# Output projection: normalized rows transposed by VectorE in squares and scaled by ScalarE, the norm's factors put into W_ff1's rows, three pairs of loads on GpSimd's queue

## The chip, the cores and the metric

One core of one Trainium2 chip runs the whole layer as a single program. The metric is the device time of one execution in microseconds. A core has five engines that run side by side and wait for each other through semaphores: TensorE (PE; PEld is its loading of weights), VectorE (DVE), ScalarE (ACT), GpSimd (POOL) and SyncE (SP). SP issues most of the DMAs, GpSimd and ScalarE some; each of the three issues them in the order of its own queue.

## The reference, cut to what matters

The model dimension is 1024, there are 2048 tokens, the MLP is 4096 wide, and all is float32.

```python
def rmsnorm(x, g):
    y = x * lax.rsqrt(jnp.mean(x * x, axis=-1, keepdims=True) + EPS)
    return y * g

# nx = rmsnorm(x, attn_norm_g); mixed = [gated linear attention ; dilated attention] of nx
h = x + einsum('bsm,md->bsd', mixed, w_out)
nm = rmsnorm(h, mlp_norm_g)
a = square(relu(einsum('bsd,df->bsf', nm, w_ff1)))
h = h + einsum('bsf,fd->bsd', a, w_ff2)
out = rmsnorm(h, final_norm_g)
```

The change touches the second and third lines: how `nm` comes from `h`, how it is turned so that the model dimension lies on the partitions, and where `mlp_norm_g` is multiplied in. Since `nm @ w_ff1` sums over the model dimension, the factor `mlp_norm_g[d]` can be applied to column d of `nm` or to row d of `w_ff1`.

## The kernel before, in words

The kernel goes through the layer in stages: input projection, both attention mixers, output projection, first MLP product (FF1), second MLP product (FF2). Two things are done in every large product. First, each float32 operand is split into a high part of type fp32r and the rest: ScalarE copies the operand into `hi`, VectorE subtracts (`split`, lines 542 to 544), and three matmuls are added up in PSUM (`mm3`, lines 139 to 142). Second, the products are not done block by block: block sums of both operands are formed, and seven block products take the place of eight (in the input projection, the output projection and FF1; FF2 has a larger scheme). The numbers j = 1 to 7 name the block products, and the tuple `order` their order.

**Output projection** (from line 1674). Two 128-token tiles make a pair p; the pairs of the first token half come first. The first four tiles are multiplied plainly (`for at in range(4)`, line 1676), the other pairs by seven block products each (`for g in range(14, 56)`, line 1709; `prep0` splits the left operand three products ahead into one of four buffers `combs0`, and `product0` multiplies and adds the result to the rows `xhs[p]` that were loaded with x). The right operands are W_out and block sums of it. `mix_wo(c)` (line 1267) loads four of those sums from `wtD` into `wtraw` in two DMAs on SP's queue and splits them.

When a tile of rows is complete, `row_done` stores it to `hD` and puts `norm_row` on a list, and after every second tile `norm_sums` as well; `next_norm` takes one of the list at fixed places of the loops. `norm_row` (lines 1410 to 1422) has ScalarE square the row into the scratch `scr` with the sum accumulated, and make 1/rms of it by two small functions (`rstd_of`). VectorE then multiplies the row in place by 1/rms and by `gM`, the factors `mlp_norm_g` spread over all partitions. TensorE transposes the eight 128x128 blocks through the identity into two PSUM banks, and ScalarE copies each bank into `bb`. `store_T` sends blocks to `hTD` on SP's queue. `norm_sums` forms the block sums of two tiles on VectorE, in place of rows that are no longer needed, and stores them too.

**The first MLP product** (from line 1887). The tokens are taken in two halves. `token_pieces` (line 1436) brings a half back from `hTD` in 14 pieces of 512 KB, always four pieces ahead, each by one DMA on SP's queue into `rb`, and splits it into the `hb` tiles: the first half while the output projection ends, the second in the middle of FF1. W_ff1 comes in 32 groups of 256 columns (16 groups, once for each half). `load_w1(g)` loads a group in two DMAs on GpSimd's queue, the first two groups at g = 49 and g = 53 of the output projection. `jobs1` lists the pairs (group, j), seven jobs a group: mostly two groups after each other, in three places two groups interleaved (`mixed`). For each job, `prep1` runs two jobs ahead: it splits a block of the weights into one of the four `combs0` and lets VectorE form the block sums; `product1` does twelve matmuls (four `mm3`) and takes the result out of PSUM, by ScalarE alone for j = 1, 6, 5 and 4, and by a VectorE sum for j = 2, 7 and 3; ScalarE then applies relu and square. `some_sums` forms VectorE's sums for FF2 and stores them to `actD`.

**What sets the order.** The order of the instructions on each engine in these stages is planned by the framework at build time: among the instructions that its model of time holds to be ready, it takes the one that was written first. A call of `keep_in_program_order` fixes an instruction behind the one that was written just before it for the same engine. Tiles named by `slot` share 25 buffers of SBUF; a new one waits until the last user of the one before it in that buffer is done.

The input projection already has what the change uses: `squares` (line 605) transposes 32x32 squares on VectorE, `both_halves` gives views of the result, `load_turned` (line 612) loads one half of a turned block by four DMAs of 32 partitions each, alternately on SP's and GpSimd's queue, and `split_turned` (line 619) splits such a piece into its place. The 32x32 squares alone do not move data between groups of 32 partitions; that is done by these loads.

Of the kernel before, what the change touches and what calls it, by code (L numbers as in the profile page):

```python
# [10 lines left out]
F32 = mybir.dt.float32  # L11
FR = mybir.dt.float32r
I32 = mybir.dt.int32
AF = mybir.ActivationFunctionType
OP = mybir.AluOpType
# [3 lines left out]
D = 1024  # L19
NT = S // 128  # L20
HT = NT // 2
CH = D // 128
# [92 lines left out]
def emit(tc, a, stop=99):  # L115
    nc = tc.nc
    V, A, G, T, SP = nc.vector, nc.scalar, nc.gpsimd, nc.tensor, nc.sync
# [6 lines left out]
    def ps(tag):  # L124
        return psum.tile([128, 512], F32, name="ps_" + tag, tag=tag, bufs=BANKS[tag])

    def slot(name, dt=F32, n=SLOT):

        return up.tile([128, SLOT], dt, name=name, tag="u", bufs=25)[:, :n]

    def view(t, shape):
        n = int(np.prod(shape))
        names = "abcd"[:len(shape)]
        return t[:, :n].rearrange(f"p ({' '.join(names)}) -> p {' '.join(names)}", **dict(zip(names, shape)))

    def bcast_row(ap, n):
        return bass.AP(tensor=ap.tensor, offset=ap.offset, ap=[[0, 128], [1, n]])
# [12 lines left out]
    ident = const.tile([128, 128], F32, name="ident")  # L150
# [69 lines left out]
    boD = [[dram.tile([S, 132], F32, name=f"boD{p}_{b}") for b in range(2)] for p in range(4)]  # L220
    mixD = dram.tile([S, D], F32, name="mixD")
    hD = dram.tile([S, D], F32, name="hD")
    hTD = dram.tile([2, 7, 128, 4, 512], F32, name="hTD")
    actD = dram.tile([NPH, 128, 8, 2, 256], F32, name="actD")
    rowD = dram.tile([8, 3, 384], F32, name="rowD")
    rbD = [dram.tile([8, 128, 384], F32, name=f"rbD{d}") for d in range(3)]
# [315 lines left out]
    def split(hi, lo, src):  # L542
        A.activation(hi, src, AF.Copy)  # L543
        V.tensor_tensor(lo, src, hi.bitcast(F32), op=OP.subtract)  # L544
# [60 lines left out]
    def squares(dst, src):  # L605

        V.transpose(dst.rearrange("p (g c t) -> p g c t", g=4, t=32), src.rearrange("p (c g t) -> p g c t", g=4, t=32))

    def both_halves(v):
        return [v.rearrange("p (g k n) -> p k g n", g=4, k=2)[:, k] for k in range(2)]  # L610

    def load_turned(dst, src, n):

        for g in range(4):
            at = bass.AP(tensor=src.tensor, offset=src.offset + 128 * g + n * 8 * 32 * 512,
                         ap=[[512, 32], [32 * 512, 8], [1, 128]])
            (SP, G)[g % 2].dma_start(view(dst[32 * g:32 * g + 32], (8, 128)), at)

    def split_turned(parts_, src, n, pin=False):

        hi, lo = [v[:, :2048].rearrange("p (c b t) -> p b c t", c=4, t=32)[:, 8 * n:8 * n + 8] for v in parts_]
        r = view(src, (8, 4, 32))
        ins = A.activation(hi, r, AF.Copy)
        if pin:
            tc.keep_in_program_order(ins)
        V.tensor_tensor(lo, r, hi.bitcast(F32), op=OP.subtract)
# [640 lines left out]
    def mix_wo(c):  # L1267

        raw = slot("wtraw")
        for k in range(2):  # L1270
            SP.dma_start(raw[:, D * k:D * k + D], wtD[c, :, D * k:D * k + D])
        for k, j in ((1, 5), (3, 6), (2, 4), (0, 7)):
            split(*block_view(j, c), raw[:, 512 * k:512 * k + 512])

# [122 lines left out]


    gs, bb = slot("gs"), slot("bb")
    gM, scr = gs[:, :D], gs[:, D:2 * D]  # L1400
    hb4 = [view(bb[:, 512 * q:], (4, 128)) for q in range(4)]
    rb, TF, TB = [], {}, {}
    norms = []

    def store_T(t, *which):
        half, i = t // HT, t % 4
        for j, q in which:
            SP.dma_start(hTD[half, j - 1][:, :, i * 128:i * 128 + 128], hb4[q] if isinstance(q, int) else q)

    def norm_row(h, t):  # L1410

        ss = stat()
        A.activation(scr, h, AF.Square, accum_out=ss)
        r = rstd_of(ss, D)
        V.scalar_tensor_tensor(h, h, r, gM, op0=OP.mult, op1=OP.mult)
        k = t % HT // 4
        for q in range(2):
            pv = view(ps("c"), (4, 128))
            for c in range(4):
                T.transpose(pv[:, c], h[:, (4 * q + c) * 128:(4 * q + c + 1) * 128], ident)  # L1420
            A.activation(hb4[2 * k + q], pv, AF.Copy)
        store_T(t, *(((1, 0), (2, 1)) if k == 0 else ((3, 3),)))

    def norm_sums(t, x):
# [11 lines left out]
    def token_pieces(half, first, pace):  # L1436

        parts_at = {}
        for n in range(14):
            parts_at.setdefault(first + n * pace // 100, []).append(n)  # L1440
        piece = lambda n: rb[n // 2 % 2][:, 1024 * (n % 2):1024 * (n % 2) + 1024]

        def load(n):
            if n < 14:
                SP.dma_start(piece(n), hTD[half, order[n // 2] - 1][:, 2 * (n % 2):2 * (n % 2) + 2].rearrange("p c s -> p (c s)"))

        def step(at):
            if at == first - 4:
                while len(rb) < 2:
                    rb.append(slot("rb"))  # L1450
                for n in range(4):
                    load(n)
            for n in parts_at.get(at, ()):
                j = order[n // 2]
                if j not in TF:
                    TF[j] = [slot(f"hb{j}", FR) for _ in range(2)]
                    TB[j] = [view(v, (4, 512)) for v in TF[j]]
                cs = slice(1024 * (n % 2), 1024 * (n % 2) + 1024)
                split(*[v[:, cs] for v in TF[j]], piece(n))
                load(n + 4)  # L1460

        return step
# [34 lines left out]
    apart = [(g, j) for g in range(2) for j in order]  # L1497
    mixed = [(0, 1), (0, 2), (0, 6), (1, 1), (0, 5), (1, 2), (0, 7), (1, 6), (0, 3), (1, 5), (0, 4), (1, 7), (1, 3), (1, 4)]
    jobs1 = [(g + n, j) for g in range(0, 2 * NP, 2) for n, j in (mixed if g in (0, NP - 2, NP) else apart)]
    raw1, acc1 = [], []  # L1500

    def load_w1(g, halves=(0, 1)):
        if g < 2 * NP:
            if len(raw1) < 2:
                raw1.append(view(slot("w1raw"), (CH, 256)))
            g0 = g % NP * 256
            for k in halves:
                G.dma_start(raw1[g % 2][:, 4 * k:4 * k + 4], w1[:, 4 * k:4 * k + 4, g0:g0 + 256])  # L1508

    def prep1(at):  # L1510

        if at >= len(jobs1):
            return
        g, j = jobs1[at]
        r = raw1[g % 2]
        (a11, a12), (a21, a22) = [[r[:, 4 * k:4 * k + 4, n * 128:n * 128 + 128] for k in range(2)] for n in range(2)]
        c = combs0[at % 4]
        split(c[:, 0], c[:, 1], {1: a11, 2: a12, 6: a11, 5: a21, 7: a11, 3: a12, 4: a22}[j])
        if j == 2:
            V.tensor_tensor(a21, a21, a22, op=OP.add)  # L1520
            V.tensor_tensor(a11, a21, a11, op=OP.subtract)
            V.tensor_tensor(a12, a12, a11, op=OP.subtract)
        if j == 6:
            V.tensor_tensor(a11, a22, a11, op=OP.subtract)
        if j in (7, 4):
            load_w1(g + 2, (0,) if j == 7 else (1,))
# [149 lines left out]
    for at in range(4):  # L1676
        p, e = divmod(at, 2)
        m = nxt
        if at == 0:
            load_x(0, True)  # L1680
            tc.keep_in_program_order(SP.dma_start(gM, bcast_row(a["mlp_norm_g"], D)))
        if at in (0, 2):
            nxt = plain_rows(p, 1)
            load_mix(p + 1)
            load_x(p + 1)
        if at == 1:
            nxt = plain_rows(1, 0)
        mix_wo(at)
        if at == 3:
            for n in range(4):  # L1690
                raw_block(2, n % 2, n // 2)
            load_mix(3)
            for g in range(14, 16):
                prep0(g)
        b = [ps("ad"[e]), ps("ad"[e])]
        parts_ = 2 if at < 2 else 1
        for q in range(parts_):
            for n in range(2):
                for c in range(q * CH // parts_, (q + 1) * CH // parts_):
                    mm3(b[n], m[:, 0, c], m[:, 1, c], *wo_part(((1, 12), (2, 3))[c // 4][n], c % 4), c == 0, c == CH - 1)  # L1700
                if q == parts_ - 1:
                    x = xhs[p][:, e, 512 * n:512 * n + 512]
                    V.tensor_tensor(x, b[n], x, op=OP.add)
        next_norm()
        row_done(p, e)
        if at == 3:
            prep0(16)
    half0, half1 = token_pieces(0, -6, 110), token_pieces(1, 7 * (NP - 2) + 3, 130)
    for g in range(14, 56):
        p, i = divmod(g, 7)  # L1710
        prep0(g + 3)
        product0(g)
        if i in (0, 1, 5):
            next_norm()
        if i == 2:
            load_x(p + 1)
            raw_block(p + 1, 0, 0)
            raw_block(p + 1, 1, 0)
        if i == 3:
            raw_block(p + 1, 0, 1)  # L1720
        if i == 4:
            raw_block(p + 1, 1, 1)
            load_mix(p + 2)
        half0(g - 56)
        if g in (49, 53):
            load_w1(int(g > 49))
        if g >= 54:
            prep1(g - 54)

    w2 = a["w_ff2"].rearrange("o (c p) n -> p (o c) n", p=128)  # L1730
# [262 lines left out]
```

## Time and profile before

| | us |
|---|---|
| median of 3 runs | 2223.89 (2220.23 to 2224.09) |
| the profiled execution | 2219.28 |
| its span | 2217.1 |
| output projection with its norms (rough, from the windows) | 855 to 1060 |
| FF1 | 1023 to 1648 |
| FF2 | 1648 to 2217 |

The profile is of one execution, and its times are counted from the start of its span. A busy time adds up the instructions of an engine with overlaps counted once. Matmuls overlap in the trace, so the step from one start to the next tells what one of them costs in TensorE's queue, and its duration does not. A row such as `L1420 PE ...` names the line in the kernel, the engine, the operation, and the tiles as out<-in. In brackets, or in lists of waits, stands who ended an engine's idle time. A helper that records all splits has one line (L543 for ScalarE, L544 for VectorE), so these are told apart by their tiles: `mcomb<-w1raw` is a split of W_ff1, `hb<-rb` one of the tokens, `wb<-wtraw` one of W_out's sums.

### The profile page before, as it was taken

What the parts mean: (1) busy time and instruction counts of PE and PEld (TensorE: products, weight loads), DVE (VectorE), ACT (ScalarE), POOL (GpSimd) and SP (SyncE); (2) the same over time, 40 slices, a digit from 0 to 9 for tenths busy, and PEclk for the clock granted to TensorE, in tenths of its full rate; (3) what the DMA queues carried; (4) which work ended last, traced back from release to release, by engine and by line L of the source; (5) the groups of instructions that cost most, each with busy time, mean ns of one, the idle gap of its engine ahead of it and who ended that gap; (6) DMA issues with size and microseconds to landing.
All of it is one profiled execution on the core that took longest, in us unless ns stands there. A gap on an engine that the chain in (4) does not pass through costs nothing.

```text
span 2217.1 us, 34928 instructions
## 1 busy us (share of the span) xinstructions
PE 2198.8 (99%) x12356; PEld 1910.1 (86%) x12356; DVE 1662.0 (75%) x3100; ACT 1231.3 (56%) x2406; POOL 604.8 (27%) x653
## 2 busy tenths in 40 slices
PE   9999999999999999999999999999999999999998
PEld 8988998899999998888888888888888888888886
DVE  8677766757777887769776778767786697576788
ACT  7364424537888884547555566555555433333446
POOL 1000300135577672000000000000008443042672
PEclk9999999999999999999999999999999999999999
DMA  6576965777967976868654456555499998677875
GB/s 208 174 218 209 253 204 187 241 243 266 313 231 229 293 262 232 264 212 273 187 167 133 150 180 182 156 177 155 133 299 279 305 297 273 213 258 244 270 263 183
DMA packets 325074, 499.88 MB, mean 225 GB/s; under 512 B 21479, under 2 KB 226938, under 8 KB 313636
## 3 DMA queue, kind: packets, MB, share of 16 engines
q1 hardware_dynamic: 285426, 336.35, 46.8%
q0 software_dynamic: 32128, 108.61, 17.2%
q10 hardware_dynamic: 7346, 52.70, 6.4%
q8 instruction: 97, 1.59, 0.3%
q14 instruction: 77, 0.63, 0.1%
HBM read 339.45 MB, written 162.85 MB: 227 GB/s over the span
## 4 chain that ended last, share of the span: by engine, by line
PE 76%; issue 12%; DMA 4%; DVE 4%; ACT 2%; POOL 1%; SPq 1%; DVEq 0%; POOLq 0%; ACTq 0%
PE ps_a L141 7%; PE ps_a L140 7%; PE ps_a L142 7%; PE ps_c L141 7%; PE ps_c L140 7%; PE ps_c L142 7%; PE ps_a L1021 4%; PE ps_d L141 4%; PE ps_d L142 4%; PE ps_d L140 4%; PE ps_o L140 3%; PE ps_o L141 3%; PE ps_o L142 3%; PE ps_d L1002 3%; PE ps_c L984 2%
## 5 line engine op out<-in xcount | busy, mean ns | idle before, releaser
L543 ACT ACTIVATE cb<-bs 128x1024 fp32r<-128x1024 f32 x104 | 110.2, 1060 | 284.4 <-PE ps_o L141 99.9
L544 DVE TENSOR_TENSOR cb<-bs,cb 128x1024 fp32r<-128x1024 f32 x104 | 150.6, 1449 | 129.0 <-ACT cb L543 128.6
L1508 POOL DMA_DIRECT2D w1raw<-w_ff x64 | 48.0, 750 | 700.3 <-DVE mcomb L544 522.7
L544 DVE TENSOR_TENSOR mcomb<-w1raw,mcomb 128x512 fp32r<-128x512 f32 x224 | 153.4, 685 | 91.4 <-ACT mcomb L543 91.4
L1798 POOL TENSOR_TENSOR bs<-bs,rb 128x1024 f32<-128x1024 f32 x60 | 167.3, 2789 | 199.9 <-DMA bs<-w_ff 196.3
L543 ACT ACTIVATE mcomb<-w1raw 128x512 fp32r<-128x512 f32 x224 | 140.5, 627 | 80.0 <-PE ps_c L142 27.3
L1021 PE MATMUL ps_a<-v,pt 128*128 128x65 f32 x1200 | 177.4, 253 | 2.5 <-ACT pt L1009 1.5
L1021 PEld LDWEIGHTS ps_a<-v,pt 128*128 128x128 f32 x1200 | 172.7, 194 | 4.3 <-ACT pt L1009 1.9
L993 ACT ACTIVATE pe<-pe,O 128x256 f32<-128x256 f32 (+1 forms) x384 | 156.2, 453 | 14.0 <-DVE O L992 11.6
L1002 PE MATMUL ps_d<-ident,pe 128*128 128x128 f32 x600 | 158.4, 279 | 0.2 <-ACT pe L993 0.2
L304 ACT ACTIVATE wcomb<-wraw 128x512 fp32r<-128x512 f32 (+2 forms) x119 | 90.3, 759 | 117.4 <-PE ps_a L141 45.5
L992 DVE CUSTOM_DVE_ANT_0 pe<-ps_c,nb 128x256 f32<-128x256 f32 (+1 forms) x384 | 126.5, 360 | 37.6 <-PE ps_d L1002 18.4
L544 DVE TENSOR_TENSOR ca<-ra,ca 128x1024 fp32r<-128x1024 f32 x84 | 133.6, 1592 | 0.2 <-ACT ca L543 0.2
L140 PE MATMUL ps_c<-hb,mcomb 128*128 128x512 f32 x320 | 124.8, 390 | 0.3 <-ACT xs L1588 0.3
L141 PE MATMUL ps_c<-hb,mcomb 128*128 128x512 f32 x320 | 124.5, 389 | 0.0
L142 PE MATMUL ps_c<-hb,mcomb 128*128 128x512 f32 x320 | 124.2, 389 | 0.0
L140 PE MATMUL ps_c<-cb,ca 128*128 128x512 f32 x312 | 121.4, 389 | 0.0
L141 PE MATMUL ps_c<-cb,ca 128*128 128x512 f32 x312 | 121.4, 389 | 0.0
L142 PE MATMUL ps_c<-cb,ca 128*128 128x512 f32 x312 | 121.4, 389 | 0.0
L1002 PEld LDWEIGHTS ps_d<-ident,pe 128*128 128x128 f32 x600 | 108.3, 185 | 0.6 <-ACT pe L993 0.3
L306 DVE TENSOR_TENSOR wcomb<-wraw,wcomb 128x512 fp32r<-128x512 f32 (+2 forms) x77 | 72.8, 945 | 48.0 <-ACT wcomb L304 47.9
L1579 ACT ACTIVATE acc<-acc 128x512 f32<-128x512 f32 x96 | 60.7, 632 | 79.5 <-DVE acc L1598 37.1
(497 smaller groups left out, 7241.5 us busy)
## 6 DMA issues: line engine op xcount, KB each, us to landing
ra<-actD ACTq DMA_DIRECT2D x50, 1024.0 KB, 7.7
actD<-ring SPq DMA_DIRECT2D x176, 256.0 KB, 3.1
rb<-w_ff POOLq DMA_DIRECT2D x84, 512.0 KB, 6.4
bs<-w_ff SPq DMA_DIRECT2D x72, 512.0 KB, 5.8
w1raw<-w_ff POOLq DMA_DIRECT2D x64, 512.0 KB, 5.2
k<-kD SPq DMA_DIRECT2D x16, 1024.0 KB, 8.0
rb<-hTD SPq DMA_DIRECT2D x28, 512.0 KB, 5.5
wraw<-w_in SPq DMA_DIRECT2D x48, 256.0 KB, 4.0
```

Source lines behind the costliest of these rows:

```text
L140: T.matmul(out, sh, mh, start=first, stop=False, **kw)
L141: T.matmul(out, sl, mh, start=False, stop=False, **kw)
L142: T.matmul(out, sh, ml, start=False, stop=last, **kw)
L304: A.activation(hi, src, AF.Copy, scale=sc)
L306: V.tensor_tensor(lo, src, hi.bitcast(F32), op=OP.subtract)
L543: A.activation(hi, src, AF.Copy)
L544: V.tensor_tensor(lo, src, hi.bitcast(F32), op=OP.subtract)
L992: V.tensor_tensor_reduce(p, s, bias, scale=1.0, scalar=BIG, op0=OP.add, op1=OP.min, accum_out=nm)
L993: A.activation(p, p, AF.Exp, bias=nm, scale=-1.0)
L1002: T.transpose(pb[:, i * 128:i * 128 + 128], src, ident)
L1021: T.matmul(self.b.opsum[:, n % 4], self.pt[:, i * 128:i * 128 + 128], self.b.v[:, blk, cols], start=first, stop=last)
L1798: (engines or ((G,), (V, V))[len(sums) - 1])[e].tensor_tensor(v, v, r, op=OP.add if op == "+" else OP.subtract)
```

## The change

1. `norm_row` no longer multiplies the row in place on VectorE, and TensorE no longer transposes it. ScalarE writes the row times 1/rms into `scr`, and `squares` has VectorE transpose it by 32x32 squares into `bb`. The two copies out of PSUM go. The four blocks `hb4` are now strided views of `bb`.
2. `hTD` is laid out by 128-token tile, so that the stores are contiguous in DRAM; a token piece is loaded by `load_turned` in four DMAs, two on SP's queue and two on GpSimd's, and split by `split_turned`.
3. `gM` and its load go. Instead `mlp_norm_g` is loaded with one value per partition and block, into the unused end of the first `w1raw`, and `scale_w1` multiplies W_ff1's rows in place on ScalarE, eight instructions of 128x256 a group, spread over the preparations of five jobs around the group's first one (from three before it to one after it). Each is fixed in program order.
4. The first two groups of W_ff1 are loaded two jobs earlier, and `prep1` is called from three jobs earlier on, for the scalings alone.
5. In `mix_wo`, three of the four pairs of loads go from SP's to GpSimd's queue.

The core of the diff:

```diff
-    hTD = dram.tile([2, 7, 128, 4, 512], F32, name="hTD")
+    hTD = dram.tile([2, 7, 4, 128, 512], F32, name="hTD")
...
-            SP.dma_start(raw[:, D * k:D * k + D], wtD[c, :, D * k:D * k + D])
+            (G if c else SP).dma_start(raw[:, D * k:D * k + D], wtD[c, :, D * k:D * k + D])
...
-    gM, scr = gs[:, :D], gs[:, D:2 * D]
-    hb4 = [view(bb[:, 512 * q:], (4, 128)) for q in range(4)]
+    scr = gs[:, :D]
+    hb4 = [v for k in range(2) for v in both_halves(bb[:, D * k:D * k + D])]
...
-            SP.dma_start(hTD[half, j - 1][:, :, i * 128:i * 128 + 128], hb4[q] if isinstance(q, int) else q)
+            SP.dma_start(view(hTD[half, j - 1, i], (4, 128)), hb4[q] if isinstance(q, int) else q)
...
-        V.scalar_tensor_tensor(h, h, r, gM, op0=OP.mult, op1=OP.mult)
+        A.activation(scr, h, AF.Copy, scale=r)
         k = t % HT // 4
-        for q in range(2):
-            pv = view(ps("c"), (4, 128))
-            for c in range(4):
-                T.transpose(pv[:, c], h[:, (4 * q + c) * 128:(4 * q + c + 1) * 128], ident)
-            A.activation(hb4[2 * k + q], pv, AF.Copy)
+        squares(bb[:, D * k:D * k + D], scr)
...
-                SP.dma_start(piece(n), hTD[half, order[n // 2] - 1][:, 2 * (n % 2):2 * (n % 2) + 2].rearrange("p c s -> p (c s)"))
+                load_turned(piece(n), hTD[half, order[n // 2] - 1], n % 2)
...
-                cs = slice(1024 * (n % 2), 1024 * (n % 2) + 1024)
-                split(*[v[:, cs] for v in TF[j]], piece(n))
+                split_turned(TF[j], piece(n), n % 2)
...
+                if not gm:
+                    gm.append(t[:, 2048:2048 + CH])
+                    SP.dma_start(gm[0], a["mlp_norm_g"].rearrange("o (c p) -> p (o c)", p=128))
...
+    def scale_w1(at):
+
+        for c, late in enumerate((-3, -2, -1, 0, -1, 0, 1, 1)):
+            if 0 <= at - late < len(jobs1) and jobs1[at - late][1] == 1:
+                r = raw1[jobs1[at - late][0] % 2][:, c]
+                tc.keep_in_program_order(A.activation(r, r, AF.Copy, scale=gm[0][:, c:c + 1]))
+
     def prep1(at):
 
-        if at >= len(jobs1):
+        scale_w1(at)
+        if at < 0 or at >= len(jobs1):
             return
...
-            tc.keep_in_program_order(SP.dma_start(gM, bcast_row(a["mlp_norm_g"], D)))
...
-        if g in (49, 53):
-            load_w1(int(g > 49))
-        if g >= 54:
+        if g in (47, 51):
+            load_w1(int(g > 47))
+        if g >= 51:
             prep1(g - 54)
```

More of the change, by code (lines that the diff above doesn't have):

```diff
@@ L1499, in emit @@
     jobs1 = [(g + n, j) for g in range(0, 2 * NP, 2) for n, j in (mixed if g in (0, NP - 2, NP) else apart)]
-    raw1, acc1 = [], []
+    raw1, acc1, gm = [], [], []
     def load_w1(g, halves=(0, 1)):
@@ L1504, in load_w1 @@
             if len(raw1) < 2:
-                raw1.append(view(slot("w1raw"), (CH, 256)))
+                t = slot("w1raw")
+                raw1.append(view(t, (CH, 256)))
+                if not gm:
+                    gm.append(t[:, 2048:2048 + CH])
+                    SP.dma_start(gm[0], a["mlp_norm_g"].rearrange("o (c p) -> p (o c)", p=128))
             g0 = g % NP * 256
```

## The prediction

> **What bounds the kernel now.** I read the page first, then busy time by windows around the change, then TensorE's instructions in order of time, then the waits. The page:
>
> ```profile
> span 2217.1 us, 34928 instructions
> PE 2198.8 (99%) x12356; PEld 1910.1 (86%) x12356; DVE 1662.0 (75%) x3100; ACT 1231.3 (56%) x2406; POOL 604.8 (27%) x653
> ```
>
> The windows (after the stretch: its length, then busy time and count of PE, PEld, DVE, ACT, POOL, then clock, DMA share, GB/s) take the output projection, its handover to the first MLP product, a steady piece of that product, and the place where its second half of tokens is loaded:
>
> ```profile
> 900.00:920.00 20.00, 19.97 (x100) 16.69 (x100) 15.32 (x24) 8.91 (x17) 0.00 (x0) 1.00 0.95 319
> 1005.00:1060.00 55.00, 54.60 (x260) 45.34 (x259) 51.89 (x70) 40.32 (x69) 5.29 (x7) 1.00 0.92 285
> 1100.00:1200.00 100.00, 100.00 (x443) 82.84 (x442) 75.62 (x154) 55.36 (x95) 8.26 (x11) 1.00 0.51 156
> 1318.00:1348.00 30.00, 29.71 (x132) 24.28 (x131) 26.16 (x39) 24.59 (x37) 2.25 (x3) 1.00 0.72 233
> ```
>
> TensorE never pauses in any of them, at full granted clock (1.00). So the end moves by what leaves TensorE's queue, minus any new pause. VectorE is the next limit at the handover (51.89 of 55) and at 1318 to 1348 (26.16 of 30), where ScalarE is close too (24.59).
>
> **What is removed from TensorE.** Each of 16 rows has eight transposes through the identity:
>
> ```profile
> 924.36 0.39 PE L140 MATMUL ps_d<-wb,mcomb 128*128 128x512 f32 x1
> 924.59 1.03 PE L1420 MATMUL ps_c<-ident,xh 128*128 128x128 f32 x8
> 925.38 0.48 PE L141 MATMUL ps_d<-wb,mcomb 128*128 128x512 f32 x1
> 925.70 0.40 PE L142 MATMUL ps_d<-wb,mcomb 128*128 128x512 f32 x1
> L1420 PE MATMUL ps_c<-ident,xh x128: 270/272/300, 870.6 to 1048.2; 128*128 128x128 f32 x128
>   DVE xh L1415: 0.7, 1
> ```
>
> Their 272 ns each are overlapping durations: 128 x 272 would be 34.8 us, but eight take 925.38 - 924.59 = 0.79 us from first start to the next matmul, and that matmul's successor starts 0.32 us after it where 0.23 is the step before (924.36 to 924.59). So a row costs 0.79 + 0.09 = 0.88, and 16 rows 14.1 us. TensorE also waits 0.7 us for the normalized row (last line). Gross gain 14.8 us. The Trainium skill's "VectorE: DVE Perf Modes", sections "The three transpose paths" and "Rules for kernel authors", prices a full 128x128 transpose at 390 ns on TensorE (bf16) and advises TensorE for it where PSUM will do, which speaks against moving it. By 390 ns per transpose the removal would be worth 49.9 us; the spacing in this trace contradicts that as a cost of the queue, and the 14.1 stand.
>
> **What takes the transposes' place.** Per row VectorE loses a scaling and gets a transpose in squares, of the kind that the input projection uses at L607; ScalarE loses two evictions and gets one scaling of 1024, whose nearest row is L1257:
>
> ```profile
> L1415 DVE SCALAR_TENSOR_TENSOR xh<-xh,stats,gs x16: 1273/1282/1285, 867.5 to 1043.2; 128x1024 f32<-128x1024 f32 x16
>   DMA hD<-xh: 12.7, 5
> L607 DVE STREAM_TRANSPOSE bp<-xp x8: 1229/1234/1240, 89.4 to 216.0; 128x1024 f32<-128x1024 f32 x8
> L1421 ACT ACTIVATE bb<-ps_c x32: 579/592/606, 871.7 to 1050.9; 128x512 f32<-128x512 f32 x32
>   PE ps_c L1420: 24.9, 9
> L1257 ACT ACTIVATE wtsum<-wtsum,stats x4: 1139/1150/1151, 522.9 to 601.2; 128x1024 f32<-128x1024 f32 x4
> ```
>
> VectorE: 16 x (1.234 - 1.282) = -0.8 us. ScalarE: 16 x 1.150 - 32 x 0.592 = -0.5 us. Both nothing. VectorE's wait of 12.7 us goes as well, since the row is no longer overwritten while its store to hD reads it; ScalarE's 24.9 us of waiting for TensorE go too. The new wait is VectorE's transpose behind ScalarE's square, two small functions and scaling; behind it on VectorE stand the projection's splits and sums, covered by four buffers of combinations. The sums of the next step read the squares with a stride, at no price I can see.
>
> At the handover cover is thin. Four of the 16 row scalings lie in 1005 to 1060, so TensorE's work shrinks there by 4 x 0.88 = 3.5 us to 51.1, while VectorE keeps 51.9. I charge 1.0 us, bounds 0 (buffers cover it) and 3.5 (nothing is gained there).
>
> **The norm's factors in W_ff1.** 32 column groups x 8 scalings of 128x256 on ScalarE, all new. The nearest form is L993, with a per-partition operand and the same shape:
>
> ```profile
> L993 ACT ACTIVATE pe<-pe,O 128x256 f32<-128x256 f32 x216 | 101.6, 500 | 10.6 <-DVE O L992 8.3 <-DVE gla L1056 0.8 <-DVE small L1057 0.6
> 663.92 0.90 ACT L993 ACTIVATE pe<-pe,O 128x256 f32<-128x256 f32 x2
> ```
>
> Two take 0.90, one 0.50: 0.40 us each in a row, 256 x 0.40 = 102 us. In 1100 to 1200 a matmul starts every 100 / 443 = 0.226 us, so a job of twelve takes 2.71 us and a group of seven jobs 19.0; ScalarE rises from 55 to 55 + 100 / 19.0 x 8 x 0.40 = 72 of 100. The sum fits; the order is the question. Each scaling is fixed behind the ScalarE instruction written before it, so the weights can no longer be prepared as far ahead as the four buffers allow. Now:
>
> ```profile
> 1101.02 0.62 ACT L543 ACTIVATE mcomb<-w1raw 128x512 fp32r<-128x512 f32 x1
> 1101.68 0.69 DVE L544 TENSOR_TENSOR mcomb<-w1raw,mcomb 128x512 fp32r<-128x512 f32 x1 [0.71 <-ACT mcomb L543]
> 1108.49 0.39 PE L141 MATMUL ps_c<-hb,mcomb 128*128 128x512 f32 x1
> 1107.49 0.68 DVE L1598 TENSOR_TENSOR acc<-ps_c,xs 128x512 f32<-128x512 f32 x1
> 1108.21 0.63 ACT L1579 ACTIVATE acc<-acc 128x512 f32<-128x512 f32 x1 [1.61 <-DVE acc L1598]
> 1108.88 0.63 ACT L1580 ACTIVATE acc<-acc 128x512 f32<-128x512 f32 x1
> ```
>
> The split is ready at 1102.37, 6.1 us before its product. Afterwards, for the second product of a group (j = 2): the last two scalings stand behind the squaring of the job three before it. From that job's last step: its drain (0.39 - 0.23 = 0.16), VectorE's sum to the first function (1107.49 to 1108.21, 0.72), that to the square (0.67) and the square (0.63) make 2.2 us, two scalings (0.40 + 0.50) 3.1, the split on ScalarE (1101.02 to 1101.68, 0.66) 3.75, on VectorE (0.69) 4.45; the product starts two jobs, 5.42 us, after it. About 1.0 us of cover is left where there were 6.1. What can use it up is a queue in front: VectorE waits for stores of the ring of sums, ten times here, up to 1.4 us:
>
> ```profile
> DVE ring L1552 <- DMA actD<-ring: 6.1, 10, 1.4
> ```
>
> I charge 2 us over the 29 ordinary groups (32 less the first and the two below); bounds 0 and 29 x 0.5 = 14.5, half the cover missed each time.
>
> Worse is 1318 to 1348, where the pieces of the second token half are split too and both first products of groups 16 and 17 come together. TensorE already waits:
>
> ```profile
> 1343.31 0.50 PE L141 MATMUL ps_a<-hb,mcomb 128*128 128x512 f32 x1 [0.29 <-DVE mcomb L544]
> ```
>
> 16 scalings, 6.4 us, must go into 30.0 - 24.59 = 5.4 us of ScalarE idleness, part of it waits. I charge half, 3.2; bounds 0 and 6.4.
>
> **Loads.** Token pieces come by four DMAs instead of one, two on SP's queue and two on GpSimd's, as at L617; three of four pairs of wtraw loads change queue:
>
> ```profile
> L1445 SPq DMA_DIRECT2D rb<-hTD x28: 319/332/682, 982.6 to 1338.3; - x28
> DMA to landing us min/median/max: 4.9/5.5/8.0
> L617 POOL DMA_DIRECT2D xp<-nTD x16: 582/583/597, 230.0 to 273.0; - x16
> DMA to landing us min/median/max: 2.4/6.9/10.6
> L1508 POOL DMA_DIRECT2D w1raw<-w_ff x64: 748/748/794, 1006.2 to 1596.9; - x64
> POOL w1raw L1508 <- DMA hTD<-xh: 156.9, 1, 156.9
>   DMA rb<-hTD: 4.5, 5
> L1271 SPq DMA_DIRECT2D wtraw<-wtD x8: 325/449/552, 841.5 to 889.3; - x8
>   DMA wtraw<-wtD: 4.8, 4
> 846.68 2.66 POOL L1079 TENSOR_TENSOR O<-O,cmb 128x512 f32<-128x512 f32 x2
> 849.84 0.95 SPq L1271 DMA_DIRECT2D wtraw<-wtD  x2
> ```
>
> GpSimd stands idle for 156.9 us up to 1006, and in 1100 to 1200 it is busy 8 of 100, so 56 issues x 0.583 = 33 us cost nothing there; landing goes from 5.5 to about 6.9. Pieces are asked for four ahead, which hides 1.4 us except in 1318 to 1348, inside the 3.2. W_ff1's first load is asked for two jobs (5.5 us) earlier, yet its buffer came free only at 1006.2, from a row's store; that store comes no later, and the first product is at 1023. The six moved wtraw loads find GpSimd idle too: its last product ends at 849.34, and the first pair that moves was issued at 849.84. ScalarE waits 4.8 us for wtraw, with TensorE running on through it; if each of the three pairs came 1.4 us later that would be 9 us, and the cover is the plain products of the first four tiles. So nothing, like the dropped load of the factors.
>
> **Sum.** 14.8 - 1.0 - 2 - 3.2 = 8.6 us off. The profiled execution took 2219.28 (span 2217.1 and 2.2 around it), so 2210.7. The three runs shown lie 0.95, 4.61 and 4.81 above it, 3.5 in the mean: I forecast 2214.2.
>
> **Rivals.**
> 1. All of it lands: every charge at its lower bound, 14.8 off, 2208.0. For it: TensorE has almost no pauses to begin with, and VectorE and ScalarE lose 37 us of waits. Against it: 1343.31 already waits.
> 2. Slower: the fixed order of the scalings makes ScalarE's chain the bound of every group. It decides once the 1.0 us of cover is short by over 0.51 us (14.8 / 29); at 1.0 us per group it is 29 + 4.2 - 14.8 = 18.4 slower, 2241. For it: cover falls from 6.1 to 1.0. Against: 28 idle points of 100 remain on ScalarE, and VectorE's waits here are mostly short.
> 3. VectorE and ScalarE give it back at the handover and at 1318 to 1348: 3.5 + 6.4 + 3 lost, 1.9 off, 2220.9.
> 4. Late token pieces. ScalarE waited five times, 4.5 us, for them; each landing 1.4 later makes 7 us more, so 1.6 off, 2221.2. The Trainium skill's "DMA: Bandwidth & Descriptors", section "SWDGE vs HWDGE vs iDMA", says that GpSimd writes its descriptors into SBUF, where VectorE in its two-port mode locks it out, and that SP's queue is immune to that: it would push every such piece this way. The issues quoted vary by only 15 and 46 ns beside a busy VectorE, so I give it little.
>
> That the edit does not do its work is hardly possible: the transposes go, and only those of the rows before the product (L1491) stay.
>
> **How the numbers follow.** Chances: forecast 0.50, rival 1 0.16, rival 2 0.13, rival 3 0.13, rival 4 0.08. About 0.2% (4.4 us) is what a measurement here tells from no change, so faster means under 2219.4. Faster: 0.47 of the forecast, 0.16, 0.05 of rival 3, 0.03 of rival 4, 0.71. Same: 0.03 + 0.08 + 0.05 + 0.01 = 0.17. Slower 0.12, nearly all rival 2. The range reaches from rival 1 less the 4 us by which runs differ, 2204, to rivals 3 and 4 plus their 7 us of unknown steady loss, 2228; outside lie rival 2 and small tails. The forecast's own range is 2208 to 2219.
>
> **What would show it.** Right: no transposes out of the rows on TensorE; VectorE transposes of 1.23 us; 256 scalings near 0.50 with 0.40 between starts; TensorE's pauses from 1060 to 1640 growing by about 5 us, most of them where the second half's pieces are split, released by VectorE's split. Wrong: pauses at j = 2 or j = 6 of every group (rival 2), TensorE idle between 990 and 1045 (rival 3), ScalarE waiting for rb above 8 us (rival 4), or a projection that is not shorter by some 12 us.

## The result and the profile after

The kernel after takes 2258.0 us (median of five runs, 2257.67 to 2262.61), the kernel before, beside it, 2223.89 (2219.25 to 2226.2). The ratio is 1.0161, 95% interval 1.0147 to 1.0175: slower by some 34 us, where 10 us faster was forecast. The profiled execution took 2258.03. From its page:

```profile
span 2256.3 us, 35097 instructions
PE 2202.1 (98%) x12228; PEld 1896.0 (84%) x12228; DVE 1656.9 (73%) x3100; ACT 1333.6 (59%) x2646; POOL 639.0 (28%) x715
L1514 ACT ACTIVATE w1raw<-w1raw 128x256 f32<-128x256 f32 x256 | 117.1, 495 | 2.1 <-DMA w1raw<-w_ff 2.1
```

TensorE has its 128 instructions fewer, VectorE is no busier, and ScalarE's busy time grows by 1333.6 - 1231.3 = 102.3 us, which is what 256 scalings were priced at (102). So nothing that was added takes long. The same windows as before:

```profile
900.00:920.00 20.00, 20.00 (x99) 16.69 (x98) 14.84 (x23) 11.00 (x21) 0.00 (x0) 1.00 0.88 320
1005.00:1060.00 55.00, 52.19 (x219) 41.88 (x218) 47.27 (x67) 46.39 (x84) 16.99 (x28) 0.97 1.01 277
1100.00:1200.00 100.00, 95.13 (x410) 75.88 (x408) 68.99 (x143) 65.73 (x125) 7.51 (x10) 1.00 0.46 139
1318.00:1348.00 30.00, 27.23 (x119) 21.89 (x117) 24.19 (x33) 26.34 (x45) 14.23 (x24) 1.00 0.90 219
```

The third line matters: in a steady piece of the first MLP product TensorE was 100.00 of 100 busy with 443 matmuls, and is 95.13 with 410, though VectorE and ScalarE have 31 and 34 idle points there. So it looks as if TensorE waits for work that comes late, not for an engine that is full. Where the time went is told by the first matmul of jobs 14, 98, 126 and 210 of that product (a job has twelve; 14 jobs are two groups) and by the first and last matmul of the second product, all from TensorE's instructions in order of time, in us:

| stage | before | after | difference |
|---|---|---|---|
| start to job 14 | 1069.6 | 1059.1 | -10.5 |
| jobs 14 to 97: 12 ordinary groups | 229.3 | 247.1 | +17.9 |
| jobs 98 to 125: groups 14 to 17 | 77.3 | 86.2 | +8.9 |
| jobs 126 to 209: 12 ordinary groups | 228.6 | 246.7 | +18.2 |
| job 210 to the second product | 29.9 | 33.0 | +3.1 |
| second product | 574.0 | 575.8 | +1.9 |

The differences are taken before rounding. The second product starts before the first one ends, so its first matmul lies inside FF1's stretch. The sum is +39.4, the two spans differ by 39.2. The transposes' gain arrived; each ordinary group lost (17.9 + 18.2) / 24 = 1.50 us. The trace shows one such loss, on TensorE and then on VectorE and ScalarE (start, us, instruction; in brackets the idle time in front and what ended it):

```profile
1116.59 0.39 PE L142 MATMUL ps_a<-hb,mcomb 128*128 128x512 f32 x1
1117.86 0.47 PE L140 MATMUL ps_a<-hb,mcomb 128*128 128x512 f32 x1 [0.88 <-DVE acc L1601]
...
1138.60 0.47 PE L140 MATMUL ps_o<-hb,mcomb 128*128 128x512 f32 x1 [1.21 <-DVE acc L1601]
...
1117.02 0.69 DVE L1601 TENSOR_TENSOR acc<-ps_a,acc 128x512 f32<-128x512 f32 x1 [0.24 <-PE ps_a L142]
1119.87 0.69 DVE L1527 TENSOR_TENSOR w1raw<-w1raw 128x512 f32<-128x512 f32 x1 [2.16 <-ACT w1raw L1514]
...
1117.75 0.63 ACT L1586 ACTIVATE acc<-acc 128x512 f32<-128x512 f32 x1 [0.63 <-DVE acc L1601]
1118.41 0.63 ACT L1587 ACTIVATE acc<-acc 128x512 f32<-128x512 f32 x1
1118.95 0.90 ACT L1514 ACTIVATE w1raw<-w1raw 128x256 f32<-128x256 f32 x2
1119.75 1.13 ACT L543 ACTIVATE mcomb<-w1raw 128x512 fp32r<-128x512 f32 x2
```

Job j = 4 starts 1117.86 - 1116.59 - 0.23 = 1.04 us late: it adds to the bank of j = 7, whose product has just ended, and VectorE's sum of j = 7 must read that bank first. The next group's j = 4 (1138.60) starts 1.37 us late in the same way, and the two alternate. In the instruction streams of before, j = 3 (and often the next group's j = 1) stands between 7 and 4. In after, the planner, which lays out the queues ahead, has TensorE take 1, 2, 5, 6, 3, 7, 4, as if the weights of j = 7 were late. The lower rows suggest a reason: the last two scalings of the next group (1118.95) come behind the function and square of the job just done, the block sum (1119.87) behind them, and splits and products behind that. In before the first block sum of a group ran far ahead of the second (L1520 at 1090.35, L1521 at 1102.40, 12 us). In after it has to wait for those scalings, and the second follows 1.8 us later (L1527 at 1119.87, L1528 at 1121.69).

### The profile page after: what moved, and what is told of

It reads as the page before. It is cut to its first block, busy times and chain, and to the rows that moved or that the text cites. A ratio compares the mean times of both kernels' runs of the same rounds, so it can differ in the third digit from the quotient of the medians.

```text
span 2256.3 us, 35097 instructions
## 1 busy us (share of the span) xinstructions
PE 2202.1 (98%) x12228; PEld 1896.0 (84%) x12228; DVE 1656.9 (73%) x3100; ACT 1333.6 (59%) x2646; POOL 639.0 (28%) x715
## 4 chain that ended last, share of the span: by engine, by line
PE 84%; DVE 5%; DMA 4%; ACT 3%; issue 3%; POOL 1%; SPq 0%; DVEq 0%; POOLq 0%; ACTq 0%
PE ps_a L140 8%; PE ps_a L141 8%; PE ps_a L142 8%; PE ps_c L140 7%; PE ps_c L141 7%; PE ps_c L142 7%; PE ps_d L140 5%; PE ps_d L141 4%; PE ps_d L142 4%; PE ps_a L1021 4%; PE ps_o L140 3%; PE ps_o L141 3%; PE ps_o L142 3%; PE ps_d L1002 3%; PE ps_c L984 2%
## 5 line engine op out<-in xcount | busy, mean ns | idle before, releaser
L544 DVE TENSOR_TENSOR cb<-bs,cb 128x1024 fp32r<-128x1024 f32 x104 | 158.7, 1527 | 131.6 <-ACT cb L543 131.5
L543 ACT ACTIVATE mcomb<-w1raw 128x512 fp32r<-128x512 f32 x224 | 136.1, 624 | 45.3 <-DVE ring L1559 18.9
L544 DVE TENSOR_TENSOR ca<-ra,ca 128x1024 fp32r<-128x1024 f32 x84 | 124.9, 1487 | 0.0
L1514 ACT ACTIVATE w1raw<-w1raw 128x256 f32<-128x256 f32 x256 | 117.1, 495 | 2.1 <-DMA w1raw<-w_ff 2.1
```

Source lines behind the costliest of these rows:

```text
L1514: tc.keep_in_program_order(A.activation(r, r, AF.Copy, scale=gm[0][:, c:c + 1]))
```

## The experiments

Four theories. A: TensorE's new order costs the time, by the bank shared between 7 and 4. B: the scalings are fixed in so late a place that the chain scaling, block sums, split is what TensorE waits for, whatever its order (rival 2 of the prediction). C: the turned loads or VectorE's squares are to blame. D: ScalarE simply has too much to do. "Two groups" below are 14 jobs, start to start, 38.1 us before and 41.2 after; "the middle" is jobs 98 to 125, 77.3 and 86.2. Each ratio is to runs of the kernel before on the same chip, whose medians were 2221.53, 2223.42 and 2221.96 us in the three series.

**Scalings away.**

```
     def prep1(at):
-        scale_w1(at)
```

> The kernel after without the 256 scalings of W_ff1 (so the norm's factors are left out of the result). In the profiles two ordinary groups of the first MLP product take 38.1 us before and 41.2 us after. Theory A (the scalings delay the weights of j = 7, so that TensorE's planned order becomes 3, 7, 4 and j = 4 has to wait for VectorE's sum of j = 7 out of the same bank): 38.1 us again, no pause at j = 4, about 2210 us (2206 to 2214), the transposes' 14.8 us less a little. Theory B (ScalarE's longer fixed chain is itself what TensorE waits for, whatever the order): the same 38.1 us and 2210. Rival C (the turned loads through GpSimd and VectorE's squares are to blame): groups stay near 41 us, above 2240 us.

Measured: 2210.6 us, ratio 0.9947 (0.9929 to 0.9965); two groups 38.1, the middle 80.3. C falls for the steady part: all of that loss comes with the scalings. The middle still loses 3.0.

**Scalings alone**, in the kernel before:

```
     def prep1(at):
+        scale_w1(at)
...
-        if g in (49, 53):
+        if g in (47, 51):
```

> The kernel before with the 256 scalings and the loads of W_ff1 two jobs earlier, and nothing else of the change (the norm's factors are thus applied twice). Theories A and B: two ordinary groups near 41.2 us, TensorE's order 3, 7, 4, about 50 us more than before, 2265 to 2280 us. Rival C: 38 to 39 us, 2224 to 2235 us.

Measured: 2283.93 us, ratio 1.0271 (1.0249 to 1.0293), a little above what was expected; two groups 41.1, the middle 92.2. The scalings, with the loads of W_ff1 two jobs earlier, make the steady loss without anything else of the change, and another 10.0 us before job 14 (it starts at 1079.7).

**TensorE's order fixed as written.**

```
     def mm3(...):
-        T.matmul(out, sh, mh, start=first, stop=False, **kw)
+        ins = T.matmul(out, sh, mh, start=first, stop=False, **kw)
+        if pin:
+            tc.keep_in_program_order(ins)
...
-                skip_group_check=True)
+                pin=c == 0, skip_group_check=True)
```

> The kernel after with the first matmul of every job of the first MLP product fixed in its place as written, so that j = 3 lies between j = 7 and j = 4; all scalings stay. Theory A: the pauses at j = 4 go, two ordinary groups take 38.1 to 39 us, 2212 to 2225 us. Theory B: TensorE pauses as long at another job, j = 7 or j = 2, because its weights come late: two groups stay at 40.5 to 42 us, 2245 to 2265 us.

Measured: 2269.76 us, ratio 1.0209 (1.0189 to 1.0228), above the range of either theory, as the middle is longer; two groups 41.3 (40.2 toward the end), the middle 94.4. Theory A falls: with j = 3 between 7 and 4 the same time is lost elsewhere. This kernel shows the chain in the open (a line number is two higher than in after: L1529, L1530 and L1531 are the block sums, L545 and L546 the split, L1561 the ring's sums). ScalarE, VectorE, TensorE:

```profile
1100.80 0.89 ACT L1516 ACTIVATE w1raw<-w1raw 128x256 f32<-128x256 f32 x2
...
1102.27 0.69 DVE L1529 TENSOR_TENSOR w1raw<-w1raw 128x512 f32<-128x512 f32 x1
1102.88 0.76 DVE L1561 TENSOR_TENSOR ring<-acc,ring 128x256 f32<-128x256 f32 x2
1103.55 0.69 DVE L546 TENSOR_TENSOR mcomb<-w1raw,mcomb 128x512 fp32r<-128x512 f32 x1
1104.15 0.69 DVE L1530 TENSOR_TENSOR w1raw<-w1raw 128x512 f32<-128x512 f32 x1
...
1104.87 0.63 ACT L545 ACTIVATE mcomb<-w1raw 128x512 fp32r<-128x512 f32 x1
...
1106.69 0.69 DVE L1531 TENSOR_TENSOR w1raw<-w1raw 128x512 f32<-128x512 f32 x1
...
1108.30 0.69 DVE L546 TENSOR_TENSOR mcomb<-w1raw,mcomb 128x512 fp32r<-128x512 f32 x1
...
1106.93 0.39 PE L140 MATMUL ps_a<-hb,mcomb 128*128 128x512 f32 x1
1109.05 0.50 PE L143 MATMUL ps_a<-hb,mcomb 128*128 128x512 f32 x1 [1.73 <-DVE mcomb L546]
```

The last two scalings end at 1101.69. The split of j = 2 (1103.55) ends at 1104.24, just in time: TensorE's second matmul of that job, the first that needs it, starts at 1104.34. That of j = 6 needs two block sums first and is done at 1108.99, 7.3 us after the scaling. Of these the chain itself takes 0.69 + 0.69 + 0.63 + 0.69 = 2.7; the rest is VectorE's queue, where ring sums, another split and the third block sum stand between the links. TensorE has the high part at 1106.93 and waits 1.89 us for the low one; the job after next (j = 7) waits 0.92.

**The same, one job earlier.** `due` is the job at which a scaling is written:

```
+                due = k + late
+                if g > 1:
+                    due = min(due, max(due - 1, jobs1.index((g - 2, (7, 4)[c // 4])) + 3))
```

> The kernel with the jobs of the first MLP product fixed as written, and the scalings up to one job (2.7 us) earlier. Its two pauses in every two groups were 1.9 and 0.9 us. If they measure how late the chain is, whatever order TensorE has: both go, two ordinary groups take 38.1 to 38.5 us, 2225 to 2240 us (the middle stays bad). Rival A' (it is the order that loses the time, and one job earlier only gives the planner the choice): 40 us or more for two groups, above 2250 us.

Measured: 2226.22 us, ratio 1.0029 (1.0016 to 1.0041); two groups 38.1, the middle 94.5. Both pauses go, with the same order and the same number of scalings. So B holds against A and D for the ordinary groups: the chain was late by less than one job. The middle stays as long as it was (94.4).

**One job earlier in the kernel after**, by the same edit, with TensorE's order left to the planner:

> The kernel after with the scalings of all column groups but the first two written up to one job (2.7 us) earlier, never sooner than three jobs behind the load of their weights. Theory B (a chain that is late by a fixed amount: with the jobs fixed in order TensorE paused twice in two groups, 1.9 and 0.9 us, both less than a job): two ordinary groups take 38.1 to 38.6 us instead of 41.2 and the time is 2216 to 2226 us. Rival D (the number of scalings on ScalarE costs it): 40 us or more for two groups, above 2245 us.

Measured: 2221.41 us, ratio 0.9989 (0.9977 to 1.0), some 37 us less than after; two groups 38.1. The middle is at 93.4: there TensorE stands still once for 13.7 us (ScalarE meanwhile waits 2.75 us for a piece and runs ten scalings before the split that TensorE needs).

```profile
1325.50 0.39 PE L142 MATMUL ps_a<-hb,mcomb 128*128 128x512 f32 x1
1339.40 0.79 PE L140 MATMUL ps_d<-hb,mcomb 128*128 128x512 f32 x1 [13.51 <-ACT mcomb L543]
```

**Three jobs earlier**, all groups but the first two, whatever the loads do (a few blocks of the groups around the middle and of group 2 are then scaled before their weights are loaded, and lack the factors):

```
...
+            late_ = late - (3 if jobs1[k][0] > 1 else 0)
...
```

> The kernel after with the scalings of all groups but the first two written three jobs earlier; the same 256 scalings, still fixed behind ScalarE's instruction before. Theories A and B (it is the lateness): the weights are split ahead again, TensorE's order is 7, 3, 4 again, two ordinary groups take 38.1 to 38.6 us, 2210 to 2222 us. Rival D (ScalarE's 72 busy of 100 and the collisions of 256 more instructions cost it, early or late): two groups stay above 40 us, above 2240 us.

Measured: 2228.39 us, ratio 1.0025 (1.0015 to 1.0036), above the range: two groups 38.1, as expected, and the middle 94.5, which was not.

**Scalings not fixed at all.**

```
-                tc.keep_in_program_order(A.activation(r, r, AF.Copy, scale=gm[0][:, c:c + 1]))
+                A.activation(r, r, AF.Copy, scale=gm[0][:, c:c + 1])
```

> The kernel after with its 256 scalings no longer fixed behind ScalarE's instruction before them: the same scalings, in an order that the planner chooses. Theory B (late because of the place in which they are fixed): two ordinary groups take 38.1 to 38.6 us, the middle is not above 45 us for two, 2212 to 2222 us. Rival D (the scalings' number costs it): still 40 us or more for two groups, above 2245 us.

Measured: 2215.18 us, ratio 0.9972 (0.9962 to 0.9982); two groups 38.1, the middle 84.3, job 14 at 1055.8. The second two groups of the middle take 46.2, a little more than the 45 that were expected. In the steady piece of its windows:

```profile
1100.00:1200.00 100.00, 100.00 (x443) 82.81 (x442) 74.17 (x151) 71.00 (x137) 8.24 (x11) 1.00 0.50 151
```

ScalarE is at 71.00 of 100, as forecast (72), and TensorE does not pause. D is gone: the work fits. One call, which fixes each scaling behind ScalarE's instruction before it, costs this kernel 2258.0 - 2215.2 = 43 us.

**Fixed and early up to group 13, free from 14**, by an edit of the kernel with all scalings one job earlier:

```
-                    tc.keep_in_program_order(A.activation(r, r, AF.Copy, scale=gm[0][:, c:c + 1]))
+                    ins = A.activation(r, r, AF.Copy, scale=gm[0][:, c:c + 1])
+                    if g < 14:
+                        tc.keep_in_program_order(ins)
```

> The scalings one job earlier and fixed up to column group 13, and not fixed from group 14 on, where the second half's pieces are split. With one job earlier throughout, two ordinary groups took 38.1 us, but the two after the middle 55.3, with TensorE idle for 13.7 us behind eight scalings that stood ahead of the splits. If their fixed place did that: 38 to 43 us there, 2206 to 2214 us, faster than both kernels. Rival: the pieces themselves are late, the pause in the middle stays above 8 us, 2216 to 2222 us.

Measured: 2219.69 us, ratio 0.9991 (0.9981 to 1.0002); the middle 86.2, its second half 45.9. The time is the rival's, the pause lies between the two: freed scalings take the middle from 93.4 to 86.2, and a pause of 4.8 us stays there.

**The pieces on SP's queue alone**, with the scalings of after, and below without them:

```
-            (SP, G)[g % 2].dma_start(...)
+            (queues or (SP, G))[g % 2].dma_start(...)
...
-                load_turned(piece(n), hTD[half, order[n // 2] - 1], n % 2)
+                load_turned(piece(n), hTD[half, order[n // 2] - 1], n % 2, (SP, SP))
```

> The kernel after with all turned loads of the token pieces on SP's queue, none on GpSimd's. Theory E (half of each piece stands on GpSimd's queue behind loads of W_ff1 that wait for their buffer, and is late where the second half's pieces are split): ordinary groups stay at 41.2 us for two, the two groups in the middle fall from 45.2 to 40 to 43 us, 2252 to 2256 us. Rival: those pieces are late for the transfer itself, or the eight scalings in a row hold ScalarE: the middle stays near 45 us, 2256 to 2260 us.

Measured: 2268.02 us, ratio 1.0197 (1.018 to 1.0214); the middle 91.2. No gain, against theory E, and the middle is longer than in after, which the rival did not say either.

**GpSimd multiplies the rows by the factors**, W_ff1 is left as it is:

```
         A.activation(scr, h, AF.Copy, scale=r)
+        G.tensor_tensor(scr, scr, gM, op=OP.mult)
...
-        scale_w1(at)
```

> The kernel after without the scalings of W_ff1; GpSimd multiplies each normalized row by the factors instead, one product of 128x1024 per row (2.76 us each by the like product on GpSimd in FF2, 16 in all), so nothing of the computation is left out. If only the scalings' lateness lost the time: two ordinary groups 38.1 us, 2208 to 2213 us, faster than both kernels. Rival F: 2.8 us more from a row's sum to its squares delays the last rows, TensorE pauses between 1010 and 1035, 2213 to 2220 us.

Measured: 2219.75 us, ratio 0.9987 (0.9972 to 1.0002). Two groups 38.1, the middle 79.1, but the first two groups 50.2. Rival F has the size; the place is another. GpSimd's queue, then ScalarE's and TensorE's:

```profile
1050.66 1.51 POOL L1508 DMA_DIRECT2D w1raw<-w_ff  x2
1052.19 2.41 POOL L1416 TENSOR_TENSOR gs<-gs 128x1024 f32<-128x1024 f32 x1
1054.52 0.79 POOL L1508 DMA_DIRECT2D w1raw<-w_ff  x1
...
1056.00 0.63 ACT L543 ACTIVATE mcomb<-w1raw 128x512 fp32r<-128x512 f32 x1 [4.07 <-DMA w1raw<-w_ff]
...
1056.69 0.51 PE L140 MATMUL ps_o<-hb,mcomb 128*128 128x512 f32 x1 [1.96 <-ACT mcomb L543]
```

The weights' loads share GpSimd's queue with the products, and ScalarE waits 4.07 us for weights, TensorE then 1.96 us for ScalarE. That is part of the 4.9 us by which these two groups are longer than without factors (45.3); smaller pauses and slower matmuls behind them make up the rest.

And the same kernel with the token pieces on SP's queue alone, by the edit above:

> The kernel with GpSimd's multiplication by rows, and with all turned loads of the token pieces on SP's queue. Theory E: the two groups after the middle take 38.2 to 39.5 us instead of the 41.6 without scalings, 2205 to 2209 us. Rival: four loads per piece on one queue are as late as before, no change against the same kernel with both queues.

Measured: 2225.12 us, ratio 1.0001 (0.9986 to 1.0016); the middle 81.5, where the same kernel with both queues has 79.1. Theory E falls a second time, although the pieces of the second half do land sooner from SP's queue alone: 5.3 us in the median and 8.3 at most, against 6.5 and 13.2.

**VectorE multiplies the rows**, norm and factors in one instruction, as before the change, and then turns them:

```
-        A.activation(scr, h, AF.Copy, scale=r)
+        V.scalar_tensor_tensor(scr, h, r, gM, op0=OP.mult, op1=OP.mult)
```

> No scalings of W_ff1; VectorE multiplies each row by its norm and the factors in one instruction (1.28 us, as before the change) into the buffer that it then turns in squares. Nothing is left out. With GpSimd's product the first two groups took 50.2 us where the kernel without factors took 45.3. If that was GpSimd's 2.8 us per row: about 46 us, 2210 to 2216 us. Rival (VectorE is the bound at the handover, 51.9 of 55 us): 16 x 1.23 us more on VectorE, a quarter of it between 1005 and 1060, lose 3 to 6 us there, 2214 to 2220 us.

Measured: 2206.38 us (2202.16 to 2207.05), ratio 0.9924 (0.991 to 0.9937): faster than both kernels, and below both ranges. The first two groups take 44.7. Its windows:

```profile
1005.00:1060.00 55.00, 54.02 (x235) 43.52 (x234) 53.64 (x79) 35.96 (x63) 16.94 (x28) 1.00 1.01 272
1100.00:1200.00 100.00, 100.00 (x443) 82.81 (x442) 71.63 (x146) 55.62 (x95) 8.23 (x11) 1.00 0.50 152
1318.00:1348.00 30.00, 27.74 (x117) 21.39 (x116) 28.03 (x52) 19.72 (x32) 4.62 (x9) 1.00 0.75 194
```

VectorE is at 53.64 of 55 at the handover, and still TensorE misses only 1 us there. Job 14 starts at 1054.4, 15.2 earlier than before; the middle takes 80.0, 2.6 more; the other stages differ by 1.2 at most. The sum is the 12.3 by which its span (2204.8) is shorter.

## Why the prediction was wrong

**The transposes: right.** 14.8 us gross were forecast; in the VectorE version the product's job 14 starts 15.2 earlier, though the new work is all there. Other pauses are in both figures, so the agreement to 0.4 us is partly luck; the spacing of matmuls was the right price, and 49.9 us was not. VectorE's and ScalarE's new row instructions cost what the rows promised, VectorE's squares a median of 1.246 us where 1.234 was taken:

```profile
L607 DVE STREAM_TRANSPOSE bb<-gs x16: 1236/1246/1248, 866.6 to 1031.7; 128x1024 f32<-128x1024 f32 x16
```

**The ordinary groups: here it failed.** The step is its account of the cover: "About 1.0 us of cover is left where there were 6.1", and from it 2 us for the 29 ordinary groups, at most 14.5. Measured: 36.1 us in 24 groups and 3.1 in the last two, beyond the upper bound. Two things in it were wrong. The cover was worked out for j = 2 alone. That split did come in time, by 0.1 us in the kernel with fixed jobs; the next links, two block sums and the split of j = 6, hang on the same last scalings and were not followed. And "a queue in front" was sized by VectorE's waits for stores, ten of up to 1.4 us, while the queue that counts is VectorE's own work: busy 70 of 100 in the kernel with fixed jobs, it had other sums and splits to do before and between the links, 4.6 us of the 7.3. So a chain of 2.7 us of instructions, which changes engine four times, took 7.3 us.

Two readings behind that step were off as well. The 6.1 us pair the split of one job with the product of another: the split that ends at 1102.37 comes just before the block sum L1521 (1102.40) that overwrites what j = 1 splits, so it is that of j = 1, and the product at 1108.49 is the j = 4 of the group before, whose result L1604 takes out at 1111.18. By the same order j = 2's split ended at 1106.86 and its product began at 1111.21, 4.35 us later. And "TensorE never pauses" was read out of windows with 54.60 of 55 and 29.71 of 30; the missing 0.4 and 0.3 us are pauses, as the row at 1343.31 says.

**Rival 2 was the right mechanism, undersized.** It had the fixed order of the scalings make ScalarE's chain the bound of every group, at 1.0 us per group, 2241 us. It was 1.50, and the scalings cost elsewhere too. Its sign, pauses at j = 2 or j = 6, showed at j = 6 (and j = 7) only where the order was fixed; in after, with the planner's order, the pause stands at j = 4. What was given against it, 28 idle points on ScalarE, was true and no argument against late links: in the steady piece ScalarE ran at 71 of 100 with the scalings freed and nothing was lost, and at 66 with them fixed, where TensorE waited.

**The handover: undersized, and the cause was another.** Charged 1.0 (up to 3.5) for VectorE; lost 14.8 - 10.5 = 4.3. VectorE is not the bound: in the last kernel it is fuller there and little is lost. In after the longest pause ends behind a queue on ScalarE, in which four scalings and two splits of tokens stand ahead of the split that TensorE waits for:

```profile
1019.70 1.05 ACT L623 ACTIVATE hb<-rb 128x1024 fp32r<-128x1024 f32 x1
1020.65 0.90 ACT L1514 ACTIVATE w1raw<-w1raw 128x256 f32<-128x256 f32 x2
1021.45 1.04 ACT L623 ACTIVATE hb<-rb 128x1024 fp32r<-128x1024 f32 x1
1022.40 0.89 ACT L1514 ACTIVATE w1raw<-w1raw 128x256 f32<-128x256 f32 x2
1023.19 1.14 ACT L543 ACTIVATE mcomb<-w1raw 128x512 fp32r<-128x512 f32 x2
```

TensorE, done with what it had at 1021.50, starts again at 1023.86, just after that split's first half. But the kernel without scalings also gains only 10.3 up to job 14, by other pauses, and the one with free scalings 13.8. So the scalings are at most one way to this loss, not the only one; that it hangs on how the queues happen to be laid out at the change of products is argued, not shown.

**The middle: undersized.** Charged 3.2 (up to 6.4), lost 8.9. Without scalings 1.7 to 3.0 are lost (three kernels with the loads of after), so by difference 6 to 7 belong to the scalings, and not to their fixed place alone: freed, they still lost 7.0 there. At 1344.10 to 1347.9 ScalarE has eight of them and one square to do, then two splits of tokens and two small functions, before the split that TensorE waits 5.1 us for. The 1.7 to 3.0 may stand with the new loads, which "So nothing" had left out, but that isn't shown. In the VectorE version ScalarE waits four times, 7.8 us, for the pieces, where it was 4.5 in five; the longest landing is 13.7 us (8.0 before):

```profile
  ACT hb L623: 7.8, 4
...
DMA to landing us min/median/max: 2.4/5.6/13.7
```

That is rival 4's sign, near its mark, in a kernel without scalings; in after itself that wait is 0.7 us, and the pieces land in 5.1 us in the median and 7.3 at most, no later than before (5.5 and 8.0). With GpSimd's product the wait was 4.7 us, hardly more than before, and 1.7 us of the middle were lost all the same. So late pieces are not shown to be what costs, and why some land late stays open: SP's queue alone made landings shorter and the time no better (1.0197 against 1.0161 with the scalings, 1.0001 against 0.9987 without, the last two within their intervals). The loads of wtraw through GpSimd were not tried by themselves.

## What to carry to other kernels

When work is put into a pipeline that runs ahead, follow the whole chain from the added instruction to every product that hangs on it, and give each link the queue of its engine; here VectorE, busy 70 of 100, made a chain of 2.7 us of instructions take 7.3. Before an instruction is fixed in a place, ask what the planner did with that freedom: here the freedom was worth 43 us, and one job earlier, still fixed, won back some 37 of them. Of three places for a factor, 16 rows on VectorE (2206.4 us) beat 256 blocks of weights on ScalarE, even unfixed (2215.2), and 16 rows on GpSimd (2219.8), though VectorE is the fullest of the three engines.

## What the runs showed of the hardware

After the pause of 5.1 us in the middle TensorE's matmuls start 0.43 us apart instead of 0.23; two windows of after, the second the piece behind the pause:

```profile
1343.00:1346.00 3.00, 3.00 (x15) 2.36 (x13) 3.00 (x5) 2.83 (x7) 1.27 (x3) 1.00 1.17 239
1351.40:1357.00 5.60, 5.60 (x13) 4.23 (x14) 5.60 (x13) 4.89 (x9) 0.00 (x0) 0.50 0.82 229
```

The granted clock is 0.50 there, so the pause cost about 13 x 0.20 = 2.6 us on top of itself. Pauses of 1.0 to 1.9 us, in every group of after and every second one with fixed jobs, were followed by no such stretch. The Trainium skill's "TensorE: Matmul & The Clock Gate", section "Why this matters for your kernels", says to leave no idle gap above about 3 us between bursts, or the clock falls to half. These two observations agree. But at the handover of after a gap of 2.36 us, with 0.3 and 0.54 more in the next two microseconds, was also followed by seven steps of 0.43 between matmuls (1026.2 to 1029.2). The gaps around it do not explain that: in the kernel after with the scalings one job earlier the same three gaps (from 1022.39) were followed by no such step, with a granted clock of 1.00, and neither was one of 3.05 us in the kernel with GpSimd's product (1008.90). In the traces of all fourteen kernels, from 842 us on, every gap of 3.5 us or more had such a stretch behind it, and no stretch stood without a gap of at least 2.1 us close in front of it; of the gaps between the two some had one and some not, and what decides there isn't shown. So the 3 us are no sharp limit here.

GpSimd's product of 128x1024 took 2.40 us in the median and up to 6.75. VectorE was busy beside the longest one (1034.14), but also all through one that took 2.41 us (981.35), so the cause stays open; a price from one row is no bound for that engine:

```profile
L1416 POOL TENSOR_TENSOR gs<-gs x16: 2382/2400/6752, 865.7 to 1052.2; 128x1024 f32<-128x1024 f32 x16
```
